# Interleaved tail convolutions, single PSUM banks, alternating product widths and four zero products in an FFN of a hybrid attention block

## The chip, the cores and the metric

The kernel runs on one core of one Trainium2 chip. The metric is device time in microseconds (us) of one execution. The engines are named as in the profile: PE (TensorE, matmul), PEld (its weight loads), DVE (VectorE), ACT (ScalarE), POOL (GpSimd) and SP (SyncE, which here issues most DMAs).

## The reference

One transformer block over 256 tokens of width 2048 in float32: three kinds of attention (forgetting, stick-breaking, memory), gated and merged, then a feed-forward part. The change touches only the feed-forward part:

```python
h2 = rms_norm(x, g_ffn[l])
u = causal_depthwise_conv(h2 @ w_up[l], conv_w[l], conv_b[l])   # 2048 -> 2 x 5632, three taps in time
u_gate, u_val = jnp.split(u, 2, axis=-1)
x = x + (jax.nn.silu(u_gate) * u_val) @ w_down[l]               # 5632 -> 2048
```

## The kernel before, in words

**Precision.** Every float32 factor is split into a high and a low part (both stored as `F32R`), and a product is taken as high x high + low x high + high x low. ACT casts the high part (L147 in the up projection, L886 in the down projection), DVE subtracts to get the low part (L148, L887).

**Up projection (L790 to L817).** The outer loop takes 11 groups of four 128-wide feature tiles (`f0`), and for each the gate half (`s = 0`) and the value half (`s = 1`): 22 rounds. A round goes over the 2048 inputs in eight pieces of two 128-deep slices. SP loads a piece of 512 KB into `raw` (four buffers), ACT and DVE make `hi` and `lo` (four buffers each). For every slice and feature tile there are two products: a long one of 512 columns (`hi` with both parts of the activations, L805) and a short one of 256 columns (`lo` with the high part, L807). So a round has 128 products. Their order within a slice is long, long, short, short for the first two tiles and the same for the other two. Results go to PSUM in pairs of two banks (`two_banks`); four pairs make up all eight banks, and a round uses two.

**Convolutions.** A round leaves two `conv` helpers, one for each pair of banks. Helpers are generators in a waiting list; `tick()` is called after each piece (and, later, after each down step), takes at most `WINDOW` of them as active, and advances each by one `yield`. `conv` has no `yield` on its way, so one `tick` puts a whole convolution into the queues of ACT and DVE: a copy out of PSUM (L734), an addition and a multiplication (L735, L736) into the one tile `u`, two activations for `y` (L739), for each of two more taps two activations for `z` and an addition (L743, L744), then SiLU for the gate half, or for the value half a product, a cast and a subtraction (L750 to L753) into `aT`, the input of the down projection.

**Weight sums.** Beside the rounds, `weight_sums` loads parts of the down weights, adds them on DVE (L770, L772, L773) and writes the sums to DRAM for later. It is advanced once a piece. Its tile `r` of 2 x 2 x 512 has two buffers.

**Down projection.** It makes the two 1024-wide halves of the output in turn (`nb`). The order of the work is written out in `PLANS`: an `e` is a pair of feature tiles multiplied plainly (two steps of 12 products, all 512 columns), an `s` is a pair done with seven products instead of eight (four steps of 3, 6, 6 and 6 products), which needs sums of weights and sums of activations (`forms`, L847 to L867, helpers too). `steps` holds for each step a preparation (load, cast, subtract) and its use on PE. The loop at the end of the function issues the preparation `AHEAD` = 2 steps ahead, then the products, then whatever is hung on that step, then a `tick`. The preparation of a later step therefore stands in ACT's and DVE's queues behind the helper parts that earlier ticks put there. `buffer` takes every third load from the ninth on from the pool that `down_pool` opens in the place of the convolutions' pools.

**Banks of the down projection.** `start(nb)` takes four pairs of banks: four banks for the plain results X and four for Y, which only the seven-product form uses. The second half takes them the other way round. `gather` (L985 to L996) adds the Y banks into the results, `results` (L1017) adds the X banks to the residual rows and issues the output DMA, and `residual` loads those rows.

## Time and profile before

| | |
|---|---|
| median of 3 runs | 1498.23 us (1496.71 to 1498.31) |
| profiled execution: time | 1497.91 us |
| profiled execution: span, first to last instruction | 1496.2 us |
| PE busy | 1482.3 us (99%), 7408 products |
| DVE busy | 1043.6 us (70%) |
| ACT busy | 862.9 us (58%) |
| up projection | 764.6 to 1256.3 us of the span |
| down projection, first half | 1256.3 to 1378.1 us |
| down projection, second half | 1378.1 to 1490.4 us |

Times in the profile count from the start of the span. A product's recorded duration overlaps that of the next, so the distance between starts tells the pace, and PE's busy share tells only where it stood still. A row of the timeline gives start, duration, engine, line, operation, output and inputs, shape and count, and in brackets the idle time of the engine before it with what ended it. A row of stretches gives the bounds, the length, then busy time and count of PE, PEld, DVE, ACT and POOL, the granted TensorE clock, the busy share of the DMA engines and GB/s. A row of the groups gives line, engine, operation, tiles, shape and count, then busy time and mean ns of one, then the engine's idle time before them.

### The profile page before, as it was taken

Reading aid. Unit: us, or ns where it says so; the run is one execution under the profiler, and the core shown is the slowest. Engines: PE = TensorE matmul, PEld = TensorE weight load, DVE = VectorE, ACT = ScalarE, POOL = GpSimd, SP = SyncE. Lnnn points to the kernel's source line nnn. Section 1 sums busy time; section 2 is a strip of 40 time slices with the busy share of each in tenths; the row PEclk is TensorE's granted clock in tenths of the full one; section 3 lists DMA queues with packets and bytes.
Section 4 is the critical chain, followed back from the end, with each engine's and each line's share of the span. In section 5 each row is a group of like instructions: output and inputs, shape, how many; then the busy total and the mean of one; then the engine's idle time right before and its main releaser. Section 6 shows DMA issues by size and latency. Waiting matters only on the chain.

```text
span 1496.2 us, 20140 instructions
## 1 busy us (share of the span) xinstructions
PE 1482.3 (99%) x7408; PEld 1250.7 (84%) x7408; DVE 1043.6 (70%) x1333; ACT 862.9 (58%) x1225; POOL 35.8 (2%) x81
## 2 busy tenths in 40 slices
PE   9999999999999999999999999999999998999998
PEld 6888888888888888888888888888888887888886
DVE  5766566555655646556557778778778776998987
ACT  6755454458544444444457667667667666655653
POOL 0000000001000000000000000000000000001000
PEclk9999999999999999999999999999999999999999
DMA  8675475475666677665676877877877774778874
GB/s 296 203 204 157 127 223 157 119 224 149 196 198 206 192 203 199 191 193 191 219 227 221 281 249 257 274 259 241 273 264 248 262 218 151 254 267 257 291 264 155
DMA packets 155921, 327.70 MB, mean 219 GB/s; under 512 B 11290, under 2 KB 20142, under 8 KB 155822
## 3 DMA queue, kind: packets, MB, share of 16 engines
q1 hardware_dynamic: 150798, 310.15, 66.3%
q0 software_dynamic: 4272, 15.21, 2.8%
q8 instruction: 58, 0.95, 0.3%
q10 hardware_dynamic: 752, 1.06, 0.2%
q14 instruction: 41, 0.34, 0.1%
HBM read 312.21 MB, written 14.16 MB: 218 GB/s over the span
## 4 chain that ended last, share of the span: by engine, by line
PE 96%; ACT 2%; DVE 1%; DMA 1%; issue 0%; POOL 0%; SPq 0%; DVEq 0%; POOLq 0%; ACTq 0%
PE u L805 22%; PE u L807 11%; PE g L158 5%; PE g L160 5%; PE g L159 5%; PE d L893 5%; PE d L891 5%; PE d L892 5%; PE s L158 2%; PE s L160 2%; PE f L158 2%; PE f L160 2%; PE s L159 2%; PE f L159 2%; PE b L160 2%; PE b L159 2%
## 5 line engine op out<-in xcount | busy, mean ns | idle before, releaser
L805 PE MATMUL u<-hT,hi_u 128*128 128x512 f32 x1408 | 442.4, 396 | 0.1
L807 PEld LDWEIGHTS u<-hT,lo_u 128*128 128x128 f32 x1408 | 264.5, 188 | 62.5
L807 PE MATMUL u<-hT,lo_u 128*128 128x256 f32 x1408 | 276.6, 278 | 0.0
L148 DVE TENSOR_TENSOR lo_u<-raw_u,hi_u 128x1024 fp32r<-128x1024 f32 x176 | 214.1, 1221 | 72.7 <-ACT hi_u L147 70.9
L147 ACT CAST hi_u<-raw_u 128x1024 fp32r<-128x1024 f32 x176 | 183.4, 1048 | 103.0 <-PE u L805 92.3
L805 PEld LDWEIGHTS u<-hT,hi_u 128*128 128x128 f32 x1408 | 214.4, 189 | 0.5 <-issue 0.5
L148 DVE TENSOR_TENSOR lo_g<-raw_g,hi_g 128x1024 fp32r<-128x1024 f32 x96 | 117.7, 1229 | 101.3 <-ACT hi_g L147 99.0
L147 ACT CAST hi_g<-raw_g 128x1024 fp32r<-128x1024 f32 x96 | 100.8, 1052 | 121.8 <-PE g L159 96.8
L158 PE MATMUL g<-hi_g,xT 128*128 128x512 f32 x384 | 150.9, 393 | 0.0
L160 PE MATMUL g<-lo_g,xT 128*128 128x512 f32 x384 | 149.6, 390 | 0.0
L159 PE MATMUL g<-hi_g,xT 128*128 128x512 f32 x384 | 149.5, 389 | 0.0
L160 PEld LDWEIGHTS g<-lo_g,xT 128*128 128x128 f32 x384 | 72.1, 188 | 15.3
L159 PEld LDWEIGHTS g<-hi_g,xT 128*128 128x128 f32 x384 | 72.2, 188 | 14.6
L158 PEld LDWEIGHTS g<-hi_g,xT 128*128 128x128 f32 x384 | 72.1, 188 | 14.5
L891 PE MATMUL d<-hi_d,aT 128*128 128x512 f32 x200 | 79.0, 395 | 4.3 <-ACT hi_d L886 4.3
L744 DVE TENSOR_TENSOR y<-y,z 128x512 f32<-128x512 f32 x88 | 60.8, 691 | 26.7 <-ACT z L743 22.9
L893 PE MATMUL d<-lo_d,aT 128*128 128x512 f32 x200 | 78.9, 395 | 0.0
L892 PE MATMUL d<-hi_d,aT 128*128 128x512 f32 x200 | 78.8, 394 | 0.0
L743 ACT ACTIVATE z<-u,taps 128x256 f32<-128x256 f32 x176 | 74.6, 496 | 0.0
L148 DVE TENSOR_TENSOR lo_s<-raw_s,hi_s 128x1024 fp32r<-128x1024 f32 (+1 forms) x40 | 44.7, 1118 | 37.2 <-ACT hi_s L147 37.1
L148 DVE TENSOR_TENSOR lo_f<-raw_f,hi_f 128x1024 fp32r<-128x1024 f32 (+1 forms) x40 | 44.7, 1120 | 34.5 <-ACT hi_f L147 33.0
L147 ACT CAST hi_f<-raw_f 128x1024 fp32r<-128x1024 f32 (+1 forms) x40 | 38.6, 967 | 52.3 <-PE f L159 47.6
(324 smaller groups left out, 2796.6 us busy)
## 6 DMA issues: line engine op xcount, KB each, us to landing
raw_u<-in_w_up_dram SPq DMA_DIRECT2D x176, 512.0 KB, 4.7
raw_g<-in_w_in_dram SPq DMA_DIRECT2D x96, 512.0 KB, 3.8
raw_d<-in_w_down_dram SPq DMA_DIRECT2D x50, 512.0 KB, 5.4
r<-in_w_down_dram SPq DMA_DIRECT2D x76, 256.0 KB, 5.6
raw_s<-in_w_down_dram SPq DMA_DIRECT2D x38, 512.0 KB, 5.2
raw_f<-in_w_in_dram SPq DMA_DIRECT2D x32, 512.0 KB, 3.6
raw_s<-in_w_in_dram SPq DMA_DIRECT2D x32, 512.0 KB, 3.6
raw_o<-in_w_out_dram SPq DMA_DIRECT2D x32, 512.0 KB, 5.0
```

The costliest lines, as they stand in the source:

```text
L147: pin(nc.scalar.copy(hi[:, :m], raw[:, :m]))
L148: pin(nc.vector.tensor_tensor(lo[:, :m], raw[:, :m], hi[:, :m].bitcast(F32), ALU.subtract))
L158: nc.tensor.matmul(o, lhsT=xh, rhs=wh, start=first, stop=False)
L159: nc.tensor.matmul(o, lhsT=xl, rhs=wh, start=False, stop=False)
L160: nc.tensor.matmul(o, lhsT=xh, rhs=wl, start=False, stop=last)
L743: nc.scalar.activation(z[:, i], u[:, i, j : j + S], AF.Copy, scale=taps_of(j, i))
L744: nc.vector.tensor_tensor(y, y, z, ALU.add)
L805: nc.tensor.matmul(ps, lhsT=hi[:, j, c], rhs=hT[:, k + j, :], start=first, stop=False)
L807: nc.tensor.matmul(ps[:, :S], lhsT=lo[:, j, c], rhs=hT[:, k + j, :S], start=False, stop=last)
L891: nc.tensor.matmul(o, lhsT=ah, rhs=w[0], start=first, stop=False)
L892: nc.tensor.matmul(o, lhsT=al, rhs=w[0], start=False, stop=False)
L893: nc.tensor.matmul(o, lhsT=ah, rhs=w[1], start=False, stop=last)
```

## The change

- `PLANS`: the first half begins with five plain pairs instead of four, and its last block has two plain pairs behind the last `s` instead of three. The numbers of `e` and `s` stay.
- The two convolutions left by the last round (`f` of 40 and 42, value half) yield five times on their way, so they are issued in six parts, and `tick` may have four active helpers from the down projection on.
- `u` becomes two tiles, used in turn by the pairs of feature tiles.
- `r` is cut in two tiles: the first with one buffer, the second with two.
- The order of the products within a slice becomes long, short, long, short.
- Ahead of the rounds 2, 7, 12 and 17 (`BEATS`, counted from 0) PE gets one more product, of the zero tile `idle` with 128 columns of itself, into the first bank that the round then begins anew.
- The pool of pairs is closed after the first half; the second half takes eight single banks.
- The forms of the first half start behind the fourth plain pair instead of the second, and the first load from the extra pool is the twelfth instead of the ninth.

```diff
--- before.py
+++ after.py
@@ -36,8 +36,9 @@
 PINNED = 1
 BLOCKS = 14
 WINDOW = 2
-PLANS = ("eeee" + "se" * 8 + "ee", "e" + "se" * 4 + "sse" + "se" * 3 + "ssee")
+PLANS = ("eeeee" + "se" * 7 + "see", "e" + "se" * 4 + "sse" + "se" * 3 + "ssee")
 AHEAD = 2
+BEATS = (2, 7, 12, 17)
 NSEVEN = tuple(plan.count("s") for plan in PLANS)
 
 
@@ -103,13 +104,13 @@
             )
 
 
-    waiting, active = deque(), []
+    waiting, active, window = deque(), [], [WINDOW]
 
     def later(gen):
         waiting.append(gen)
 
     def tick():
-        while waiting and len(active) < WINDOW:
+        while waiting and len(active) < window[0]:
             active.append([waiting.popleft(), 0])
         for a in list(active):
             if a[1] > 0:
@@ -701,7 +702,8 @@
 
 
     ppx.close()
-    pp2.append(ctx.enter_context(tc.tile_pool(name="pp2", bufs=4, space=bass.MemoryType.PSUM, reuse_waits="tile")))
+    pp2x = ctx.enter_context(ExitStack())
+    pp2.append(pp2x.enter_context(tc.tile_pool(name="pp2", bufs=4, space=bass.MemoryType.PSUM, reuse_waits="tile")))
 
     def two_banks(name):
         return pp2[0].tile([P, 2, 512], F32, tag="pair", name=name)
@@ -720,20 +722,25 @@
         xrs.close()
         sp = side.enter_context(tc.tile_pool(name="sp", bufs=2, reuse_waits="tile"))
         cp = uv.enter_context(tc.tile_pool(name="cp", bufs=4, side="right", reuse_waits="tile"))
-        u = cp.tile([P, 2, S + 2], F32, tag="u", bufs=1, name="u")
-        nc.vector.memset(u[:, :, 0:2], 0.0)
-        cps.extend((cp, u, sp))
+        us = [cp.tile([P, 2, S + 2], F32, bufs=1, name=f"u{i}") for i in range(2)]
+        for u in us:
+            nc.vector.memset(u[:, :, 0:2], 0.0)
+        cps.extend((cp, us, sp))
 
     def scratch(name):
         return sm.tile([P, 512], F32, tag="junk", bufs=2, name=name).rearrange("p (i s) -> p i s", i=2)
 
     def conv(ps, f, s):
-        cp, u, _ = cps
+        cp, us, _ = cps
+        u = us[f // 2 % 2]
         taps_of = lambda j, i: taps[:, j, s * FT + f + i : s * FT + f + i + 1]
+        tail = f >= FT - 4 and s == 1
         cr = scratch(f"cr_{f}_{s}")
         nc.scalar.copy(cr, ps[:, :, S:])
         nc.vector.tensor_tensor(cr, cr, ps[:, :, :S], ALU.add)
         nc.vector.tensor_tensor(u[:, :, 2:], cr, rbc.unsqueeze(1).to_broadcast([P, 2, S]), ALU.mult)
+        if tail:
+            yield
         y = cp.tile([P, 2, S], F32, tag="y", name=f"y_{f}_{s}")
         for i in range(2):
             nc.scalar.activation(y[:, i], u[:, i, 2:], AF.Identity, scale=taps_of(2, i), bias=taps_of(3, i))
@@ -742,39 +749,47 @@
             for i in range(2):
                 nc.scalar.activation(z[:, i], u[:, i, j : j + S], AF.Copy, scale=taps_of(j, i))
             nc.vector.tensor_tensor(y, y, z, ALU.add)
+            if tail:
+                yield
         if s == 0:
             nc.scalar.activation(y, y, AF.Silu)
             ys[f] = y
         else:
             g = ys.pop(f)
             nc.vector.tensor_tensor(g, g, y, ALU.mult)
+            if tail:
+                yield
             a = aT[:, f : f + 2]
             nc.scalar.copy(a[:, :, :S], g)
+            if tail:
+                yield
             nc.vector.tensor_tensor(a[:, :, S:], g, a[:, :, :S].bitcast(F32), ALU.subtract)
-        return
-        yield
-
+            ended.append(f)
+
+    ended = []
     made = {}
     asked = [(0, p) for p in range(NSEVEN[0])] + [(1, p) for p in range(NSEVEN[1])]
 
     def weight_sums(nb, p):
         n0 = nb * PIECE
-        r = cps[2].tile([P, 2, 2, 512], F32, tag="r", name=f"r_{nb}_{p}")
+        r = [
+            cps[2].tile([P, 2, 512], F32, tag=f"r{j}", bufs=1 + j, name=f"r{j}_{nb}_{p}") for j in range(2)
+        ]
         for j, n in ((0, 1), (0, 0), (1, 1), (1, 0)):
             tc.keep_in_program_order(
-                nc.sync.dma_start(r[:, j, n], dv[:, 2 * p + j, n0 + n * 512 : n0 + (n + 1) * 512])
+                nc.sync.dma_start(r[j][:, n], dv[:, 2 * p + j, n0 + n * 512 : n0 + (n + 1) * 512])
             )
             yield 1
         yield 1
-        b01 = r[:, 0, 1]
-        tc.keep_in_program_order(nc.vector.tensor_tensor(r[:, 0, 0], r[:, 0, 0], b01, ALU.add))
+        add = lambda o, i: tc.keep_in_program_order(nc.vector.tensor_tensor(o, o, i, ALU.add))
+        add(r[0][:, 0], r[0][:, 1])
         yield 1
-        tc.keep_in_program_order(nc.vector.tensor_tensor(r[:, 1, 1], r[:, 1, 1], r[:, 0, 0], ALU.add))
-        tc.keep_in_program_order(nc.vector.tensor_tensor(r[:, 1, 0], r[:, 1, 0], r[:, 1, 1], ALU.add))
+        add(r[1][:, 1], r[0][:, 0])
+        add(r[1][:, 0], r[1][:, 1])
         T = dram.tile([P, PIECE], F32, name=f"T_{nb}_{p}")
         made[nb, p] = T
         yield 2
-        nc.gpsimd.dma_start(T, r[:, 1].rearrange("p b n -> p (b n)"))
+        nc.gpsimd.dma_start(T, r[1].rearrange("p b n -> p (b n)"))
 
     adding = []
 
@@ -792,13 +807,17 @@
         for s in range(2):
             pairs = [two_banks(f"u{f0 + i}_{s}") for i in (0, 2)]
             c0 = s * D_FF + f0 * P
+            if f0 // 2 + s in BEATS:
+                tc.keep_in_program_order(
+                    nc.tensor.matmul(pairs[0][:, 0, :128], lhsT=idle[:, :P], rhs=idle[:, :128], start=True, stop=True)
+                )
             if asked and f0 // 2 + s > 0:
                 adding.append([weight_sums(*asked.pop(0)), 0])
             for k in range(0, KT, 2):
                 hi, lo = piece(upv[:, k : k + 2, c0 : c0 + 512], 2, 512, f"u{f0}_{s}_{k}")
                 for j in range(2):
                     first, last = k + j == 0, k + j == KT - 1
-                    for i, part in ((0, hi), (1, hi), (0, lo), (1, lo), (2, hi), (3, hi), (2, lo), (3, lo)):
+                    for i, part in ((0, hi), (0, lo), (1, hi), (1, lo), (2, hi), (2, lo), (3, hi), (3, lo)):
                         ps = pairs[i // 2][:, i % 2]
                         c = slice(i * P, (i + 1) * P)
                         if part is hi:
@@ -819,6 +838,7 @@
 
     def down_pool():
         if not dn:
+            assert len(cps) == 3 and len(ended) == FT // 2
             uv.close()
             side.close()
             dn.append(ctx.enter_context(tc.tile_pool(name="dn", bufs=4, side="right", reuse_waits="tile")))
@@ -870,7 +890,7 @@
 
     def buffer(name):
         turn[0] += 1
-        if turn[0] > 8 and turn[0] % 3 == 0:
+        if turn[0] > 10 and turn[0] % 3 == 0:
             return down_pool().tile([P, PIECE], F32, tag="more", bufs=2, name=name)
         return wp.tile([P, PIECE], F32, tag="raw", name=name)
 
@@ -998,12 +1018,15 @@
     banks = {}
 
     def start(nb):
-        b = [two_banks(f"d{nb}_{i}") for i in range(4)]
-        if nb:
-            b = b[2:] + b[:2]
-        X = [[b[t][:, n] for n in range(2)] for t in range(NT)]
-        Y = [b[2 + i // 2][:, i % 2] for i in range(4)]
-        banks[nb] = X, Y
+        if nb == 0:
+            pairs = [two_banks(f"d{nb}_{i}") for i in range(4)]
+            b = [pair[:, i] for pair in pairs for i in range(2)]
+        else:
+            pp2x.close()
+            pp3 = ctx.enter_context(tc.tile_pool(name="pp3", bufs=8, space=bass.MemoryType.PSUM, reuse_waits="tile"))
+            b = [pp3.tile([P, 512], F32, tag="bank", name=f"d{nb}_{i}") for i in range(8)]
+            b = b[4:] + b[:4]
+        banks[nb] = [[b[2 * t + n] for n in range(2)] for t in range(NT)], b[4:]
 
     def results(nb):
         for t in range(NT):
@@ -1041,12 +1064,13 @@
                 n_done += 1
                 if n_done == 4:
                     at(len(steps) - 1, lambda nb=nb: residual(nb))
-                if formed < ns and n_done >= 2:
+                if formed < ns and n_done >= 4 - 2 * nb:
                     at(len(steps) - 2, lambda p=formed: later(forms(p)))
                     formed += 1
         assert s == ns and not straight and formed >= ns
         at(len(steps) - 1, finish)
         at(len(steps) - 1, lambda nb=nb: results(nb))
+    window[0] = 4
     for f in after_step.pop(-1):
         f()
     for prep, _ in steps[:AHEAD]:
```

## The prediction

> **What bounds the kernel now.** I read the page's engine shares first, then busy time by stretches, then the timeline where TensorE's share dips, then the waits.
>
> ```profile
> PE 1482.3 (99%) x7408; PEld 1250.7 (84%) x7408; DVE 1043.6 (70%) x1333; ACT 862.9 (58%) x1225; POOL 35.8 (2%) x81
> ...
> 788.11:1256.27 468.16, 468.16 (x2691) 408.48 (x2690) 366.07 (x433) 326.69 (x506) 10.71 (x20) 1.00 0.76 251
> 1256.27:1274.58 18.31, 13.98 (x50) 10.53 (x49) 13.41 (x21) 11.84 (x23) 1.64 (x3) 0.82 0.38 121
> 1274.58:1378.06 103.48, 103.48 (x457) 85.66 (x456) 94.85 (x133) 59.17 (x72) 1.09 (x2) 1.00 0.76 259
> 1378.06:1490.44 112.38, 112.36 (x496) 92.72 (x494) 97.39 (x119) 62.93 (x70) 3.29 (x6) 1.00 0.71 244
> 1490.44:1496.20 5.76, 0.00 (x0) 0.00 (x0) 1.35 (x3) 0.00 (x0) 0.00 (x0) 0.74 0.34 113
> ```
>
> Each stretch gives its length, then busy time of PE, weight loads, DVE, ACT, POOL, and the granted clock. TensorE is busy throughout the up projection (row 1) and most of the down projection (rows 3, 4). It stands still only at the seam between them (row 2) and after its last product (row 5). Elsewhere the time is the number of products times their spacing, and only a changed spacing can move it. The spacing is read from starts:
>
> ```profile
> 525.68 0.39 PE L158 MATMUL g<-hi_g,xT 128*128 128x512 f32 x1
> ...
> 590.28 0.39 PE L158 MATMUL g<-hi_g,xT 128*128 128x512 f32 x1
> ...
> 296.71 0.28 PE L160 MATMUL s<-lo_s,xT 128*128 128x256 f32 x1
> ...
> 297.43 0.28 PE L160 MATMUL s<-lo_s,xT 128*128 128x256 f32 x1
> ...
> 788.11 0.62 PE L805 MATMUL u<-hT,hi_u 128*128 128x512 f32 x2
> ```
>
> - Long products alone: 285 spacings from 525.68 to 590.28, 226.67 ns each. Short ones alone: six from 296.71 to 297.43, 120 ns. The difference of 256 columns is 106.67 ns, so a product costs 0.4167 ns a column and 13.33 ns besides.
> - Up projection, order long, long, short, short: 21 rounds of 32 groups of four from 788.11 to 1256.27, 696.67 ns a group, 348.33 per long and short. The columns are 640 ns, so the fixed part is 14.17 ns a product.
>
> **The seam.**
>
> ```profile
> 1256.27 0.40 PE L891 MATMUL d<-hi_d,aT 128*128 128x512 f32 x1
> ...
> 1264.21 0.39 PE L893 MATMUL d<-lo_d,aT 128*128 128x512 f32 x1
> 1268.89 0.79 PE L891 MATMUL d<-hi_d,aT 128*128 128x512 f32 x1 [4.29 <-ACT hi_d L886]
> ...
> 1270.15 0.79 PE L893 MATMUL d<-lo_d,aT 128*128 128x512 f32 x1
> ...
> 1277.42 0.39 PE L891 MATMUL d<-hi_d,aT 128*128 128x512 f32 x1
> ...
> 1255.77 0.59 ACT L734 COPY cr<-u 128x512 f32<-128x512 f32 x1 [1.27 <-PE u L807]
> ...
> 1267.27 0.62 ACT L752 CAST aT<-y 128x512 fp32r<-128x512 f32 x1 [1.49 <-DVE y L750]
> 1267.80 2.94 ACT L886 CAST hi_d<-raw_d 128x1024 fp32r<-128x1024 f32 x3
> ```
>
> The last two convolutions (f = 40 and 42, second half) go to ACT's queue whole, from 1255.77 to 1267.89, ahead of the cast for the fourth down step. Three steps were cast ahead; they last 36 products, until 1264.44. The fourth starts at 1268.89, 4.45 late; a product then waits for its low part (1270.15), and the granted clock of the stretch until 1274.58 is 0.82, against 1.00 before and after. Step 6 should start 60 products after 1256.27, at 1269.87, and starts at 1277.42: **7.55 us lost**, and nothing after wins it back.
>
> **The change, part by part.** The sum is made against the profiled execution, 1497.91 us (its span 1496.2 and 1.7 around it); the median of the three runs is 0.3 above.
>
> *Convolutions in steps.* Each of the two is cut in six parts, one a step, both at a time (at most four helpers run), so a cast waits for one part of each. A step of PE is 12 x 0.2267 = 2.72, and three are cast ahead (8.17).
>
> ```profile
> L743 ACT ACTIVATE z<-u,taps 128x256 f32<-128x256 f32 x176 | 74.6, 496 | 0.0
> ...
> L887 DVE TENSOR_TENSOR lo_d<-raw_d,hi_d 128x1024 fp32r<-128x1024 f32 x50 | 59.2, 1219 | 7.0 <-ACT hi_d L886 6.9
> ...
> L739 ACT ACTIVATE y<-u,taps 128x256 f32<-128x256 f32 x88 | 48.2, 595 | 12.0 <-DVE u L736 12.0
> ...
> L735 DVE TENSOR_TENSOR cr<-cr,u 128x512 f32<-128x512 f32 x44 | 30.1, 685 | 12.9 <-ACT cr L734 12.9
> ...
> L855 DVE TENSOR_TENSOR fd<-aT 128x512 f32<-128x512 f32 x11 | 7.5, 684 | 0.0
> ...
> L867 DVE TENSOR_TENSOR aT<-fr,aT 128x128 fp32r<-128x128 f32 x11 | 3.1, 284 | 0.0
> ```
>
> ACT's costliest part is 4 activations of L739 and 4 of L743 beside a cast of 1.05, some 5 us once; the next has 3.0, the rest less: inside the 8.17. DVE is the tighter queue. Twelve operations of 0.69 (L735) are 8.3 us. Up to the second step of the first seven-product block DVE also has 7 low parts of 1.22, two of a block (0.69 and 1.22), and two sets of forms (seven operations from L855 to L867, 2.95 in all, of the second set the first 2.1: the forms now start two pairs later, after the convolutions): 23.8 us, from 1256.39 to 1280.2, perhaps 1281 with its waits. That step is due at 1256.27 + 10 x 2.72 + 0.68 = 1284.2. So the new order (five plain pairs first) holds by 3 us; four further operations and two casts leave about 1.5 at that block's end. **-7.55.** If a wait comes back it is here.
>
> *The clock there.* The half-speed stretch follows a wait of 4.45. The Trainium skill ("TensorE: Matmul & The Clock Gate", What's actually happening) gives the window of idling that halves the clock as about 3.4 us, and the trace agrees. By it a remaining wait under 3.4 would cost only itself, a longer one some 3 more.
>
> *Single banks.* For the second half the pairs of banks become eight banks.
>
> ```profile
> 1487.74 1.28 DVE L1017 TENSOR_TENSOR xr<-xr,d 128x512 f32<-128x512 f32 x2
> ...
> 1488.68 0.39 PE L893 MATMUL d<-lo_d,aT 128*128 128x512 f32 x1
> ...
> 1490.04 0.39 PE L893 MATMUL d<-lo_d,aT 128*128 128x512 f32 x1
> 1490.46 1.35 DVE L1017 TENSOR_TENSOR xr<-xr,d 128x512 f32<-128x512 f32 x3 [1.43 <-PE d L893]
> ```
>
> DVE idles 1.43 and then adds three results, though the first of them, bank (1,0), has its last product at 1488.68, 1.36 before that of (1,1). With a bank of its own it is added in that gap, and the end has one 512-wide addition fewer: **-0.69**. The output DMA then goes sooner too; the three are no longer issued together. Between the halves TensorE runs through (row 1274.58:1378.06), so finer banks win nothing. The first half's last block has one plain pair fewer behind it, and its gathering moves 5.4 later, in front of the second half's first low parts on DVE; 103.48 - 94.85 = 8.6 us of slack in that stretch hide it.
>
> *Smaller tiles.* The weight-sum buffers become one of the first kind and two of the second, u becomes two tiles.
>
> ```profile
> 952.58 0.43 SPq L765 DMA_DIRECT2D r<-in_w_down_dram  x1
> ...
> 957.29 0.69 DVE L772 TENSOR_TENSOR r<-r 128x512 f32<-128x512 f32 x1
> ...
> ACT hi_u L147 <- PE u L805: 92.3, 62, 2.1
> ```
>
> The transfer issued at 952.58 must now wait until the sum before has been read, 957.98: SP stands 5.4 us, and behind it the next raw pieces. In 62 cases the cast waits for a product to free its buffer, not for data; casts so run up to three pieces (3 x 2.79 us) ahead of their products. Zero; were that cover gone, up to 5.4 a round in 18 rounds.
>
> *Long and short in turn.* 1408 pairs change neighbours; numbers, banks' order at a round's end and loads stay. No row shows this order. Two shorts in a row and two longs in a row go; each load of weights now has the other length beside it. Streams of one length have 13.33 ns fixed, this mixture 14.17. Bounds: a stream just disturbed is slower.
>
> ```profile
> 725.07 0.38 PE L195 MATMUL hT<-ident,xres 128*128 128x128 f32 x2
> ...
> 725.52 0.39 PE L159 MATMUL o<-hi_o,mT 128*128 128x512 f32 x1
> ...
> 726.91 0.39 PE L159 MATMUL o<-hi_o,mT 128*128 128x512 f32 x1
> ...
> 509.75 0.39 PE L159 MATMUL g<-hi_g,xT 128*128 128x512 f32 x1
> 509.97 0.39 PE L160 MATMUL g<-lo_g,xT 128*128 128x512 f32 x1
> ```
>
> Six spacings from 725.52 are 231.7 ns: fixed part 18.3, so 2816 x 4.2 ns = +11.8 us. The shortest single one, near 224 ns (0.22 from 509.75), has 10.7: 2816 x -3.5 = -9.8. Nearest are the settled streams, so I take the pair as 226.67 + 120 = 346.67: 1408 x -1.67 = **-2.35**.
>
> For the same step the Trainium skill ("TensorE: Matmul & The Clock Gate", Back-to-back issue gap) gives an isolated product its columns at 2.4 GHz and about 2.5 ns, so an estimate by it is 324.9 a pair and -33 us. The trace speaks against it here, with 13.33 besides the columns for both lengths.
>
> *Zeros.* Four products of 128 columns, each before a round's first, on a bank that that product waits for anyway.
>
> ```profile
> 701.75 1.03 PE L195 MATMUL hT<-ident,xres 128*128 128x128 f32 x8
> ...
> 702.85 0.39 PE L159 MATMUL o<-hi_o,mT 128*128 128x512 f32 x1
> ```
>
> Eight foreign 128-column products and one long take 1.10 us: 0.109 each after 0.227. Four: **+0.44**, from 0.27 (128 x 0.4167 + 13.33 each) to 0.65 with eleven disturbed spacings behind each. They may also move the stream from one spacing to another; that is in the bounds above.
>
> Sum: 1497.91 - 7.55 - 0.69 - 2.35 + 0.44 = **1487.8**.
>
> **The rivals.**
> - *A shorter spacing.* A load beside a product of the other length hides better, or the zeros put the stream on its short spacing. For: single spacings of 224; the fixed part depends on what went before. Against: no steady row below 13.33. 1490.1 - 9.8 = 1480.3.
> - *The order changes nothing.* TensorE pays per load, and loads stay; the mixture keeps 14.17 or a little more: 1490.1 to 1492.5.
> - *Never settled (slower than before).* Change of length at every product keeps the stream at 231.7's fixed part in all 22 rounds: 1490.1 + 11.8 = 1501.9. It decides from 8.2 - 0.4 = 7.8 us, 2.8 ns a product. For: the mixture already pays more than streams of one length, and it changes length half as often. Against: that is only 0.83 more.
> - *The seam still waits.* DVE has 1.5 us to spare at the first block; a return of 2 gives 1489.8, with all of 4.45 left 1492.2.
> - *The fixed part goes.* If a load beside the other length were hidden whole, 2816 x 14.17 = 39.9 would go: 1450. Against: long products alone, with twice the time for a load, still pay 13.33. The skill's gap, above, would be this case.
>
> **How the numbers follow.** About 0.2% (3.0 us) is what a measurement here can tell from no change. Forecast 0.38 (its own range 1486 to 1489.5); shorter spacing 0.21 (1478 to 1486); nothing from the order 0.18; seam 0.09; never settled 0.06, between it and no loss (1493 to 1500) 0.06; the fixed part gone 0.02. Faster takes the forecast, the shorter, the unchanged, the seam and the last, less a little where the seam's rest is longest: 0.88; same 0.07; slower 0.05. The range goes from 1479 (the shortest spacing and a little) to 1494 (today's spacing with a rest of the seam): it leaves out the unsettled cases and the last.
>
> **What would show it.** The fourth down step starts at 8.2 us after the first, PE clock 1.00 in that stretch; after the last product two additions of 0.33 and none of 0.69; a round of 22.19 us against 22.29 (22.4 and more for the slower rival, 21.85 for the shorter). SP's r transfers start later, with no gap on PE. It would be wrong if a round's length moved by over 0.2 us, or if DVE's low parts came late at the first block.

## The result and the profile after

The changed kernel takes 1495.74 us (median of 20 runs, 1490.33 to 1498.11) against 1498.04 before: a ratio of 0.9983 with an interval of 0.9976 to 0.9990, 2.3 us. Forecast were 1487.8, and 1479 to 1494 as range. The profiled execution took 1495.4, its span 1493.7.

The stretches of the changed kernel; the columns are those of the table of before. The up projection is cut where zeros stand (rounds 2, 7, 12 and 17), the down projection at its tenth step, at the last 24 products of the first half, and at the end.

```profile
PE 1484.5 (99%) x7412; PEld 1251.4 (84%) x7412; DVE 1042.5 (70%) x1334; ACT 861.6 (58%) x1225; POOL 35.7 (2%) x81
...
788.14:810.37 22.23, 22.23 (x132) 19.34 (x130) 16.60 (x19) 16.92 (x26) 0.56 (x1) 1.00 0.59 163
810.37:921.43 111.06, 111.06 (x644) 97.02 (x643) 88.38 (x107) 76.49 (x121) 2.66 (x5) 1.00 0.79 258
921.43:1034.62 113.19, 113.19 (x644) 98.12 (x643) 87.26 (x104) 76.86 (x121) 2.65 (x5) 1.00 0.81 266
1034.62:1147.82 113.20, 113.20 (x645) 98.01 (x643) 89.50 (x107) 77.64 (x121) 2.66 (x5) 1.00 0.79 255
1147.82:1258.84 111.02, 111.02 (x643) 97.12 (x643) 83.93 (x97) 77.73 (x121) 3.77 (x7) 1.00 0.76 244
1258.84:1286.06 27.22, 27.22 (x122) 22.53 (x121) 24.64 (x38) 18.01 (x30) 0.00 (x0) 1.00 0.61 202
1286.06:1367.66 81.60, 81.60 (x361) 67.59 (x360) 76.13 (x107) 51.24 (x62) 0.00 (x0) 1.00 0.75 259
1367.66:1382.55 14.89, 12.90 (x50) 9.79 (x48) 12.40 (x18) 3.74 (x4) 4.37 (x8) 0.89 0.76 226
1382.55:1489.46 106.91, 106.91 (x472) 88.21 (x470) 92.60 (x113) 60.71 (x68) 0.00 (x0) 1.00 0.70 241
1489.46:1493.70 4.24, 0.01 (x1) 0.00 (x0) 0.75 (x2) 0.00 (x0) 0.00 (x0) 0.77 0.43 141
```

Four things are to be seen.
- **The seam is closed.** Ten down steps take 27.22 us, 120 products of 0.2267, at a clock of 1.00: the 7.55 us are back.
- **The up projection has two lengths of round.** 111.06 and 111.02 us for five rounds at both ends (22.2 each), 113.19 and 113.20 for the ten in the middle (22.6 each). TensorE is busy throughout in both. From round 1 on it takes 470.70 us where the old order took 468.16: 2.5 more, not 2 less.
- **A new gap** lies in the row from 1367.66, where the second half of the down projection starts: PE busy 12.90 of 14.89, clock 0.89. Its products one by one, and what DVE did:

```profile
1372.88 0.39 PE L913 MATMUL d<-lo_d,aT 128*128 128x512 f32 x1
1375.25 0.47 PE L911 MATMUL d<-hi_d,aT 128*128 128x512 f32 x1 [1.99 <-DVE xr L1040]
...
1376.95 0.63 PE L912 MATMUL d<-hi_d,aT 128*128 128x512 f32 x1
...
1378.23 0.63 PE L912 MATMUL d<-hi_d,aT 128*128 128x512 f32 x1
...
1379.33 0.40 PE L912 MATMUL d<-hi_d,aT 128*128 128x512 f32 x1
...
1367.14 0.68 DVE L1007 TENSOR_TENSOR xr<-xr,d 128x512 f32<-128x512 f32 x1
...
1373.22 0.69 DVE L1016 TENSOR_TENSOR xr<-xr,e 128x512 f32<-128x512 f32 x1
1373.83 2.47 DVE L1040 TENSOR_TENSOR xr<-xr,d 128x512 f32<-128x512 f32 x4
```

The second half's first product waits 1.99 us for the first half's results (L1040), which DVE adds only after the whole gathering (L1007 to L1016). By the trace it starts at 1375.25, right behind the second of the four result additions (ended at 1375.11), and the fourth product at 1376.36, right behind the last (1376.30). The next nine spacings are 0.31 to 0.59 us, where 0.23 is the rule; for 3.41 us of them the granted clock is 0.50:

```profile
1375.68:1379.09 3.41, 3.41 (x10) 2.24 (x9) 3.41 (x6) 0.00 (x0) 1.91 (x5) 0.50 0.87 300
```

Between the first down product's start and the last one's lie 230.25 us, 4.0 more than without this gap (below).
- **The end** is 4.6 us from the last product's start (1489.08) to the end of the span; before it was 6.2. DVE's last work:

```profile
1486.64 1.28 DVE L1040 TENSOR_TENSOR xr<-xr,d 128x512 f32<-128x512 f32 x2
1488.15 0.69 DVE L1040 TENSOR_TENSOR xr<-xr,d 128x512 f32<-128x512 f32 x1 [0.23 <-PE d L913]
1489.51 0.75 DVE L1040 TENSOR_TENSOR xr<-xr,d 128x256 f32<-128x256 f32 x2 [0.67 <-PE d L913]
```

The third 512-wide addition now lies ahead of the last product's end. The books of the span: +2.5 (up projection) -7.55 (seam) +4.0 (gap) -1.5 (end) = -2.5, from 1496.2 to 1493.7.

### The profile page after: what moved, and what is told of

Same layout as the page of the kernel before. It is cut to its first block, busy times and chain, and to the rows that moved or that the text cites. A ratio compares the mean times of both kernels' runs of the same rounds, so it can differ in the third digit from the quotient of the medians.

```text
span 1493.7 us, 20178 instructions
## 1 busy us (share of the span) xinstructions
PE 1484.5 (99%) x7412; PEld 1251.4 (84%) x7412; DVE 1042.5 (70%) x1334; ACT 861.6 (58%) x1225; POOL 35.7 (2%) x81
## 5 line engine op out<-in xcount | busy, mean ns | idle before, releaser
L824 PE MATMUL u<-hT,hi_u 128*128 128x512 f32 x1408 | 493.4, 396 | 0.1
L826 PE MATMUL u<-hT,lo_u 128*128 128x256 f32 x1408 | 392.7, 279 | 0.0
L824 PEld LDWEIGHTS u<-hT,hi_u 128*128 128x128 f32 x1408 | 264.3, 188 | 63.6 <-issue 0.5
```

The costliest lines, as they stand in the source:

```text
L824: nc.tensor.matmul(ps, lhsT=hi[:, j, c], rhs=hT[:, k + j, :], start=first, stop=False)
L826: nc.tensor.matmul(ps[:, :S], lhsT=lo[:, j, c], rhs=hT[:, k + j, :S], start=False, stop=last)
```

## The experiments

Medians are told with the lowest and highest run. The kernel before had medians of 1497.3 to 1498.3 beside them. A profile shows one execution of each kernel; what the others did is known by their times alone.

### The gap between the halves

`right_banks`: the eight banks come from three pools, meant to give X of the second half the banks that Y of the first half had.

```
-  pp3 = ... tile_pool(name="pp3", bufs=8, ...)
-  b = [pp3.tile(...) for i in range(8)]
-  b = b[4:] + b[:4]
+  b = {}
+  for name, of in (("pp3a", (4, 5)), ("pp3", (0, 1, 2, 3)), ("pp3b", (6, 7))):
+      pool = ... tile_pool(name=name, bufs=len(of), ...)
+      for i in of: b[i] = pool.tile(...)
```

> The changed kernel, but the second half's eight single banks come from three pools, so that its X results fall on the banks that held the first half's Y, which the gathering frees first. Theory: TensorE's late start of the second half (2.15 us idle, then half clock, 4.0 us in all) is a wait for banks that the last results of the first half still read. Then no wait at that place, the granted clock is 1.00 there, and the time falls by 4.0 from the changed kernel's: 1491.7 at the median. Rival: the start is late because the gathering and the results have moved behind two more steps on DVE, whatever the banks; then half of the 2.15 or more stays.

1491.64 (1487.88 to 1492.76), a ratio of 0.9953 (0.9940 to 0.9966). The same stretch:

```profile
1367.80:1382.60 14.80, 14.80 (x67) 12.24 (x66) 14.34 (x20) 6.82 (x8) 4.38 (x8) 1.00 0.73 213
```

TensorE runs through, clock 1.00; from the first down product to the last it is 226.24 us, 4.0 less; the rounds of the up projection are the changed kernel's. Nothing but the handing out of banks differs, so the gap is a matter of which banks come first. In the changed kernel the second half's first products fall on banks that the results read, behind the whole gathering; that follows from the additions which release them (above). By which rule the one pool hands out its banks, no run here shows.

### The order alone, and all but the order

`turn_only` is the kernel before with the one line of the order changed. `old_order` is the changed kernel with the old order and no zeros; `right_old` the same with the right banks.

```
-  ((0, hi), (1, hi), (0, lo), (1, lo), (2, hi), (3, hi), (2, lo), (3, lo))
+  ((0, hi), (0, lo), (1, hi), (1, lo), (2, hi), (2, lo), (3, hi), (3, lo))
```

> The kernel before with only the order of products changed to long, short in turn. Theory A: each execution falls into one of the two spacings after the last disturbance in round 0 and keeps it: 1497.9 - 2.3 = 1495.6 or 1497.9 + 6.7 = 1504.6, every round alike. By the forecast made before the change was seen: always 1495.6. Rival B (other work decides): both kinds of round within one execution, without zeros.

> The changed kernel with the products in the old order (long, long, short, short) and without zeros. If the order alone made the rounds uneven, every round is back to 22.29 us, the seam's 7.55 us and the end's 1.5 stay won, and the 4.0 us lost at the start of the second half stay lost: 1497.9 - 7.55 - 1.5 + 4.0 = 1492.9, with little spread between executions. If rival B (the held loads) slows rounds, rounds 7 to 16 are longer than 22.29 here too.

> The changed kernel with the banks of the second half handed out so that its first matmuls fall on banks that come free first, the order of before (two long, two short) and no zeros: the seam, the small tiles and the single banks without the order. All rounds at 22.29 us as with the old order before, no gap in the down projection: 1492.3 - 4.0 = 1488.3, and little scatter. If the old order too can be thrown into a slower spacing by late pieces (theory L, in this order not seen so far), rounds of 22.5 and more and up to 4 us more.

`turn_only`: 1495.66 (1494.94 to 1496.42), ratio 0.9984 (0.9976 to 0.9993). All rounds are 22.19 us:

```profile
810.34:921.27 110.93, 110.93 (x642) 97.00 (x641) 89.15 (x107) 77.79 (x121) 2.67 (x5) 1.00 0.80 270
...
1143.14:1254.07 110.93, 110.93 (x642) 97.03 (x641) 83.85 (x97) 77.83 (x121) 2.15 (x4) 1.00 0.72 231
```

A pair takes 110.93 / 320 = 346.67 ns, the forecast value. `old_order`: 1492.34 (1491.54 to 1494.27), 0.9965 (0.9953 to 0.9976), all rounds 22.29. The gap is still there, with the same wait, but the clock stays at 1.00:

```profile
1373.48 0.47 PE L911 MATMUL d<-hi_d,aT 128*128 128x512 f32 x1 [1.99 <-DVE xr L1040]
...
1374.58 0.50 PE L911 MATMUL d<-hi_d,aT 128*128 128x512 f32 x1 [0.17 <-DVE xr L1040]
...
1371.10:1385.00 13.90, 11.74 (x51) 9.11 (x50) 11.96 (x16) 6.81 (x8) 4.37 (x8) 1.00 0.78 227
```

From the first down product to the last it takes 228.95 us here, 2.7 more than without the gap. So of the changed kernel's 4.0 us some 2.7 are the waits, and the other 1.3 the half clock. `right_old`: 1489.25 (1488.92 to 1489.88), 0.9944 (0.9933 to 0.9956), 1.0 above what was expected; with 2.7 for the gap in place of 4.0 the expectation would have been 1489.6. In its profile the waits of the cast for raw pieces (sum, times, longest), the up projection and ten down steps:

```profile
ACT hi_u L148 <- DMA raw_u<-in_w_up_dram: 46.8, 18, 3.9
...
788.97:1257.13 468.16, 468.16 (x2690) 408.48 (x2689) 365.35 (x433) 323.78 (x506) 12.32 (x23) 1.00 0.78 253
1257.13:1284.40 27.27, 27.27 (x123) 22.58 (x122) 24.72 (x38) 18.05 (x31) 0.00 (x0) 1.00 0.61 200
```

Seam and end without order and zeros are worth 9.05 by the trace (7.55 + 1.5); the medians of `right_old` and of the kernel before beside it differ by 8.5. So the order alone brings what was forecast, and seam and end alone bring what the traces show. What is lost in the up projection appears only with the new order, what is lost between the halves only with the new pool.

### The zeros

`no_zeros` is the changed kernel with an empty list of rounds; `turn_zeros` is `turn_only` with the zeros at 2, 7, 12 and 17.

> The changed kernel without the four zero products; the rest stays. In the changed kernel's trace the rounds 1 to 6 and 17 to 20 last 22.19 us and the rounds 7 to 16 last 22.61 to 22.69, and each jump falls on a round with a zero product. Theory A: the alternating stream has two steady spacings, 346.7 and 353.3 ns per long and short, a disturbance decides which one it falls into, and it then stays; the zeros only draw again. Then all rounds from 1 to 21 have one length, 22.19 or 22.61, with no jump at 7 or 17, and single executions differ by up to 21 x 0.42 = 9 us: near 1491 or near 1500. Rival B: the slow rounds come from other work in those rounds (the held loads of the weight sums). Then rounds 7 to 16 stay slow and the time stays near 1495. Rival C: the zeros keep the stream fast for some rounds and without them all are slow: always 1500.

> The kernel before with the order in turn and the zeros ahead of rounds 2, 7, 12 and 17, and nothing else. If the zeros themselves draw the spacing anew (theory Z), some of the stretches 2-6, 7-11, 12-16 and 17-20 run at 22.6 us a round: 5 x 0.42 = 2.1 us more for each, so 1496.1 to 1504. If they only cost their own 0.44 us and the spacing stays (rival): 22.19 in all rounds, 1496.1. Theory L says nothing against either, but with two buffers no waits of the cast for raw pieces are expected in this kernel.

`turn_zeros`: 1500.47 (1499.63 to 1501.54), 1.0018 (1.0010 to 1.0027), where the order alone gave 0.9984. Its stretches are the changed kernel's:

```profile
811.31:922.38 111.07, 111.07 (x645) 97.03 (x643) 89.17 (x107) 77.82 (x121) 2.67 (x5) 1.00 0.80 270
922.38:1035.56 113.18, 113.18 (x644) 98.09 (x643) 87.15 (x103) 78.27 (x121) 2.66 (x5) 1.00 0.79 258
1035.56:1148.76 113.20, 113.20 (x645) 98.03 (x643) 89.27 (x107) 78.36 (x121) 2.66 (x5) 1.00 0.77 256
1148.76:1259.78 111.02, 111.02 (x643) 97.12 (x643) 83.88 (x97) 77.90 (x121) 2.16 (x4) 1.00 0.72 228
```

The four zeros themselves cost 0.13 us each; ten rounds of 0.43 more are the rest of 4.8. In the starts of the products there are two patterns. The shorter repeats after two pairs: intervals of 231, 112, 233 and 117 ns, 693.33 together (346.67 a pair). The longer repeats after three: 241, 120, 236, 113, 233 and 117, 1060 together (353.33 a pair). Nothing waits in either. The zeros of round 7 in the changed kernel, one after the other:

```profile
920.70 0.39 PE L824 MATMUL u<-hT,hi_u 128*128 128x512 f32 x1
...
921.04 0.40 PE L824 MATMUL u<-hT,hi_u 128*128 128x512 f32 x1
...
921.39 0.23 PE L812 MATMUL u<-idle 128*128 128x128 bf16 x1
921.43 0.48 PE L824 MATMUL u<-hT,hi_u 128*128 128x512 f32 x1
...
922.57 0.40 PE L824 MATMUL u<-hT,hi_u 128*128 128x512 f32 x1
...
922.93 0.40 PE L824 MATMUL u<-hT,hi_u 128*128 128x512 f32 x1
```

A single distance tells little: long products lie 343 and 350 ns apart in turn in the shorter pattern, and 361, 349 and 350 in the longer one. The 0.36 from 922.57 to 922.93 is one that only the longer one has, and it comes back every third time from there on.

`no_zeros`: 1495.63 (1490.72 to 1499.67), 0.9980 (0.9967 to 0.9993): taking the zeros out of the changed kernel wins nothing in the median, and the runs scatter by 9 us. Theory A had foretold that scatter, but one length for all rounds in an execution; in the profile the rounds change length where no zeros stand:

```profile
ACT hi_u L148 <- DMA raw_u<-in_w_up_dram: 66.3, 22, 4.5
...
789.05:947.34 158.29, 158.29 (x898) 137.35 (x897) 121.73 (x145) 108.64 (x170) 3.75 (x7) 1.00 0.76 242
...
992.26:1103.20 110.94, 110.94 (x643) 97.82 (x642) 88.84 (x107) 76.49 (x121) 2.66 (x5) 1.00 0.79 260
...
1148.31:1261.38 113.07, 113.07 (x643) 98.10 (x641) 83.80 (x97) 77.42 (x121) 3.77 (x7) 1.00 0.77 248
...
1114.29 0.39 PE L824 MATMUL u<-hT,hi_u 128*128 128x512 f32 x1
1114.53 0.39 PE L826 MATMUL u<-hT,lo_u 128*128 128x256 f32 x1
1114.75 0.39 PE L824 MATMUL u<-hT,hi_u 128*128 128x512 f32 x1
```

The first line is of the waits (sum, times, longest): the cast waits 22 times for a raw piece, 66.3 us, in `turn_only` 3 times and 5.4. Rounds 1 to 7 take 22.61 us, rounds 10 to 14 22.19, rounds 16 to 20 22.61; the changes lie in rounds 8 and 15. The last three lines show the second one, the start of the fifth piece of round 15: a short product lasts 0.39 where 0.28 is usual, its weight load has waited 0.16 us for DVE's low part, and from there on the longer spacing holds. In round 8 the change to the shorter spacing lies at the start of the fifth piece too, where the load of a low part comes 0.06 us later than usual. In round 9 a stop of 0.2 us at the same place changed nothing. All three times the cast had waited 3.9 to 4.6 us for a raw piece some 7 us before. So not only zeros, but a brief stop for a late piece can change the spacing too, in either direction, and need not. Between the two changes the intervals are 230 and 117 ns in turn: the shorter spacing has a pattern of one pair as well.

What rule do the zeros follow? Two kernels were made for the idea that those of odd rounds turn the spacing: `turn_zero7`, `turn_only` with zeros at 7 alone, and `turn_even`, at 2 and 12.

> The kernel before with the order in turn and one matmul of 128 zeros, ahead of round 7 alone. Theory Z (a stop of the stream picks the spacing anew, and the zeros of an odd round turn the one spacing into the other, as the traces of the three kernels with zeros show at 7 and 17, those of an even round do not): rounds 1 to 6 at 22.19 us, 7 to 20 at 22.6: 14 x 0.42 = 5.9 us more than the order alone for one matmul of a tenth of a microsecond, 1501.7. Rival (the slow rounds of those kernels have another cause, and the zeros only lie beside it): all rounds at 22.19, 1495.8.

> The kernel before with the order in turn and the zeros ahead of rounds 2 and 12 alone. Theory Z as told: those of an even round keep the spacing, all rounds at 22.19 us, 1495.7 + 0.2 = 1495.9. If any zeros may turn the spacing (rival), rounds at 22.6 from 2 or from 12 on: 1499.7 to 1503.9.

Both came out the other way round. `turn_zero7` has no long round: 1496.20 (1494.51 to 1497.33), 0.9991 (0.9982 to 1.0000). `turn_even` turns at 12: 1499.99 (1499.30 to 1501.16), 1.0017 (1.0008 to 1.0026). Its rounds 2 to 11 and 12 to 21:

```profile
811.08:1033.08 222.00, 222.00 (x1284) 193.97 (x1283) 176.40 (x210) 155.76 (x241) 5.34 (x10) 1.00 0.79 266
1033.08:1259.29 226.21, 226.21 (x1283) 196.09 (x1282) 173.15 (x204) 156.61 (x241) 4.82 (x9) 1.00 0.74 240
```

The idea of odd rounds falls. What fits all of these is that the place in the pattern decides. The shorter pattern of two pairs has two places: a round begins with 233, 117 (a) or with 231, 112 (b). Zeros lead from a to b, and from b into the longer pattern. From there the long interval that ends the round decides: after 236 the longer pattern stays, after 241 the stream goes back to b. `turn_zeros34` and `turn_zeros278` (zeros at 3 and 4; at 2, 7 and 8) were made to break this.

> The kernel before with the order in turn and zeros ahead of rounds 3 and 4 alone. Theory P (the stream stands at a place of its pattern; the first zeros lead from the one place of the shorter spacing to the other, the second from there to the longer spacing, whatever the round): rounds 1 to 3 at 22.19 to 22.27 us, 4 to 20 at 22.6: 1495.7 + 0.2 + 17 x 0.42 = 1503.0. Rival (which round has the zeros decides, and only those of 7 or 12 with one before were seen to turn it): all rounds at 22.2, 1495.9, or only one of the two zeros turns it: 1503.4 from round 3 on.

> The kernel before with the order in turn and zeros ahead of rounds 2, 7 and 8. Theory P: as with four zeros the second, at 7, brings the longer spacing, and round 7 ends at the place of its three (the long interval of 240 ns last) at which round 16 ended there, where the next zeros led back: round 7 at 22.7, all others at 22.19 to 22.27: 1495.7 + 0.3 + 0.5 = 1496.5. Rival (zeros lead back at random, or only after more rounds): 7 to 20 at 22.6, 1495.7 + 0.3 + 14 x 0.42 = 1501.9.

Both came out as the theory of places says, with one thing that it left open (below). `turn_zeros34`: 1503.43 (1502.59 to 1506.23), 1.0046 (1.0029 to 1.0063), long from round 4 on. `turn_zeros278`: 1496.89 (1495.57 to 1498.04), 0.9993 (0.9984 to 1.0003). Of the second, round 1, rounds 2 to 6, round 7, and rounds 8 to 21:

```profile
788.50:811.15 22.65, 22.65 (x131) 19.55 (x130) 16.60 (x19) 16.91 (x26) 0.56 (x1) 1.00 0.65 198
811.15:922.22 111.07, 111.07 (x645) 97.03 (x643) 89.27 (x107) 77.92 (x121) 2.67 (x5) 1.00 0.81 268
922.22:944.95 22.73, 22.73 (x131) 19.63 (x131) 16.61 (x19) 15.59 (x25) 0.53 (x1) 1.00 0.80 266
944.95:1255.65 310.70, 310.70 (x1795) 271.75 (x1794) 243.68 (x288) 218.33 (x337) 6.95 (x13) 1.00 0.76 249
```

This execution started in the longer spacing, which was not expected; the zeros of 2 led it back (from 233 as last long interval, a case not seen before), those of 7 away, those of 8 back again. The profiled executions of all kernels with zeros hold 22 of them, and all 22 fit the rule with 233 added to it. Why the place decides, the runs don't show.

### The smaller tiles, and how the stream starts

`turn_small` is `turn_only` with the change's smaller tiles of the weight sums. `two_r_y3` is the changed kernel with the right banks, no zeros, and two buffers of either tile (room from the y of the convolutions).

```
-  cps[2].tile([P, 2, 512], F32, tag=f"r{j}", bufs=1 + j, ...)
+  cps[2].tile([P, 2, 512], F32, tag=f"r{j}", bufs=2, ...)
...
-  y = cp.tile([P, 2, S], F32, tag="y", ...)
+  y = cp.tile([P, 2, S], F32, tag="y", bufs=3, ...)
```

> The kernel before with two things of the change: the order of long and short matmuls in turn, and the smaller tiles of the weight sums (one buffer for the two rows that are read first). No zeros, no convolutions in steps, pairs of banks in both halves. Theory L (the single buffer holds the queue of the loads, pieces of the up projection come late now and then, and a late piece throws the stream from the spacing of 346.67 ns a pair to that of 353.33): some rounds at 22.6 us, waits of the cast for the raw piece in the up projection in tens of us where the kernel with the order alone has next to none, time between 1497 and 1504 and scattered from run to run. Rival C (the slow spacing comes with the convolutions in steps or their window): all 20 rounds at 22.19 us, 1495.7 as with the order alone.

> The changed kernel with the banks of the second half handed out so that the first matmuls of it fall on banks that come free first, no zeros, and two buffers for both tiles of the weight sums (the room for it taken from the convolution's y, three buffers in place of four). Theory L: no late pieces, all rounds at 22.19 us; against the version with the right banks (1491.6, with ten rounds 0.43 longer and 0.44 us of zeros) 4.3 + 0.4 less: 1486.9, between 1486 and 1488. Rival C (the slow spacing comes with the convolutions in steps): ten to twenty rounds at 22.6, 1491 to 1496. If three y are too few, the convolutions are late and the last ones show at the seam: up to 2 us more in either case.

`turn_small`: 1500.65, ratio 1.0014 (1.0000 to 1.0028), but no run lies there: six lie between 1495.22 and 1498.07, six between 1503.24 and 1504.24. `two_r_y3`: 1487.36, 0.9945 (0.9927 to 0.9963); six from 1486.57 to 1487.70, two at 1496.10 and 1496.77, and the profiled execution is one of these two:

```profile
789.27:1264.15 474.88, 474.88 (x2690) 411.89 (x2689) 366.12 (x433) 330.20 (x506) 12.32 (x23) 1.00 0.76 249
...
ACT hi_u L148 <- DMA raw_u<-in_w_up_dram: 0.3, 1, 0.3
```

These are 21 rounds of 22.61 us, with one late piece, by 0.3 us. The profiled execution of `turn_small`, of its slower group, has the longer spacing in all 21 rounds too (474.87 us), though the cast waits 12 times there. So the theory that late pieces bring the longer spacing holds only in part: they change it on the way (`no_zeros`), but the stream can also come out of round 0 in it, where TensorE waits for its first pieces, and then keep it to the end. In eleven runs each, `turn_only` and `turn_zeros` showed no second group, though the profiled `turn_zeros278`, the same kernel up to round 2, did start in the longer spacing; why some kernels start in either and others do not stays open.

The changed kernel has late pieces as well: its cast waits 15 times, 34.4 us. In its profiled execution the spacing changes at zeros alone. That the late pieces make the scatter of its other runs (1490.33 to 1498.11, where `turn_zeros`, without the smaller tiles, has 1499.63 to 1501.54) is likely, but not shown.

### Versions beyond the change

`two_r_quad` is `two_r_y3` with four long and then four short products; `two_r_zero7` and `two_r_zero2` are `two_r_y3` with zeros at 7 or at 2 alone.

> The version with the right banks, two buffers for both tiles of the weight sums and no zeros, with four long matmuls and then four short ones in place of long and short in turn. Theory of the spacing: each order has its own; two and two gave 348.33 ns a pair, in turn 346.67 or 353.33. If the spacings of 226.67 (long after long) and 120 (short after short) hold and only the two changes of length cost something, four and four has fewer changes and one steady spacing near 346.7 to 347.5: 22.19 to 22.24 us a round, 1487 to 1488, without the runs at 1496. If a change from short to long is what makes the phase ambiguous, two spacings stay.

> The version with the right banks, two buffers for both tiles of the weight sums, the order in turn, and zeros ahead of round 7 alone. Without zeros its runs fell into two groups, 1487 (six) and 1496.4 (two). Theory Z: the zeros of round 7 turn either spacing into the other: runs that begin in the shorter one end at 1487.1 + 0.1 + 14 x 0.42 = 1493.1, runs that begin in the longer one at 1496.4 + 0.1 - 14 x 0.42 = 1490.6; none at 1487 or at 1496.4. Rival (zeros pick at random): runs at all of these, 1487.2, 1490.6, 1493.1 and 1496.5.

> The version with the right banks, two buffers for both tiles of the weight sums and the order in turn, with zeros ahead of round 2 alone. Its runs without zeros were 1486.6 to 1487.7 (six) and 1496.1 to 1496.8 (two, in the longer spacing from round 0 on; these end round 1 at the place, last intervals 236, 114, 232, from which the zeros of round 2 led back in the kernel with zeros at 2, 7 and 8). Theory P: a start in the shorter spacing goes to its other place and stays, 1487.0 + 0.1 = 1487.1; a start in the longer one goes back at round 2, 1487.1 + 0.3 + 0.5 = 1487.9; no run at 1496, median 1487.1 to 1487.6. Rival (at random): some runs at 1496.5.

`two_r_quad`: 1492.54 (1492.04 to 1492.83), 0.9967 (0.9955 to 0.9979): one spacing, but 22.45 us a round, 350.8 ns a pair; the hope of 22.19 fell. `two_r_zero7`: 1487.35, all five runs from 1486.93 to 1487.59, 0.9931 (0.9919 to 0.9944); in the profile its zeros found place a and led to b, where a turn to the longer spacing was expected. `two_r_zero2`: 1486.97, five runs from 1486.26 to 1487.25 and one at 1495.64, 0.9937 (0.9919 to 0.9955):

```profile
788.23:810.46 22.23, 22.23 (x131) 19.32 (x130) 16.59 (x19) 16.92 (x26) 0.56 (x1) 1.00 0.64 192
810.46:1254.28 443.82, 443.82 (x2563) 388.14 (x2562) 349.44 (x414) 311.58 (x481) 11.77 (x22) 1.00 0.78 257
```

These are 20 rounds of 22.19 in the profiled execution. The long run at 1495.64 goes against the theory as told, which had none at 1496; the rival, that zeros pick at random, had some. That run was not profiled; a start in place b would do it by the theory, and that is only argued. In the median all of these beat both kernels. Of the versions without zeros, `right_old` and `two_r_quad` showed no second group, in five and six runs; `right_old` is 1.9 us behind `two_r_zero7`, whose five runs are too few to rule one out.

## Why the prediction was wrong

- **Seam: right.** -7.55 forecast and measured, and the clock there is 1.00. DVE's low parts lead their products by 1.53 us at the least in the first block, where 1.5 was worked out.
- **Order: right by itself.** 346.67 ns a pair in `turn_only`, as forecast; from round 1 on its up projection is 2.2 us shorter. The step took this as the one settled spacing, and here the error lies; the stream has a second one, 353.33, which lies inside the step's bounds and above the old 348.33. Held for all rounds it makes the order a loss of 1408 x 5.0 ns = 7 us.
- **Zeros: the step that failed first.** Their own price was nearly right (0.13 each for 0.11 forecast). "They may also move the stream from one spacing to another; that is in the bounds above" named the mechanism, but the sum gave it nothing, and the one rival that used it had them win (the "short spacing"). `turn_zeros` against `turn_only` shows it as a loss of 10 x 0.43 = 4.3 us, and the changed kernel's profile has the same ten rounds. The zeros are not the only thing that can do it: `no_zeros` has long rounds too, from its start and from late pieces. The chance of 0.06 for 1493 to 1500 stood for a stream that changes of length keep unsettled; `turn_only` shows that they don't, and that the time fell near there is luck.
- **Single banks between the halves: the second.** "Between the halves TensorE runs through, so finer banks win nothing" asked only what they can win. That the new pool hands out other banks first was not looked at; it costs 4.0: some 2.7 of waiting and 1.3 of the clock behind it. The 8.6 us of slack did not help: the wait is for the order of DVE's work, not for its amount.
- **The clock rule.** From the Trainium skill ("TensorE: Matmul & The Clock Gate", What's actually happening) the prediction took that a wait under some 3.4 us would cost only itself. The 1.99 us here were followed by 3.41 us at half speed, and so in `no_zeros`; in `old_order` the same wait left the clock at 1.00. So a wait below 3.4 us can cost more than itself, and the measurement decides; what tells the two cases apart, no run here shows.
- **Single banks at the end: the mechanism right, the term too small**, 1.5 for 0.69. From the last product's start to the end of the additions 0.6 went (1.77 to 1.18); from there to the end of the span 0.9 (4.39 to 3.44), the output that "goes sooner too" and was not priced.
- **Smaller tiles: zero as a wait, not zero as a disturbance.** The cast did wait for raw pieces, and with the old order the rounds never showed it: `right_old` has 18 such waits, 46.8 us, and the up projection takes 468.16 as before. With the order in turn the brief stops that come through can change the spacing.

From 1487.8 to the profiled 1495.4: +4.3 (spacing) +4.0 (banks) -0.8 (end) = +7.5; the last 0.1 is the zeros' own price and rounding. Of the two signs that it named, "if a round's length moved by over 0.2 us" is what the profile showed (22.6 against 22.29); the other, late low parts at the first block, did not come.

## What to carry to other kernels

Where TensorE is full, the length of a stream is the number of its products times a spacing, and the spacing can have more than one steady value: look at the length of each round before and after every stop, and at runs that fall in groups, before a median is believed. A stop of a tenth of a microsecond cost four here; whoever puts something into a steady stream should measure it alone and in two places. When tiles move to another pool, work out which buffer the first use gets, and who reads that buffer last.

## What was not expected of the hardware

- In-turn products of 512 and 256 columns have two steady spacings, 346.67 and 353.33 ns a pair, with the same instructions and no wait in either. These are 52 and 53 times 6.667 ns; the streams of one length, 226.67 and 120, are 34 and 18 times the same. The 348.33 of two and two and the 350.8 of four and four are not multiples of it. Whether there is such a step, the runs don't tell.
- A stream keeps its spacing for hundreds of microseconds (474.88 us in `two_r_y3`), and the effect of a 128-column product depended on where in a pattern of two or three pairs it fell.
- After 1.99 us without a product, the granted clock was halved for 3.41 us in two profiled executions (the changed kernel and `no_zeros`) and not at all in a third (`old_order`).
